# Moving a pool of late buffers by 128 bytes, and the weights of one kind of matmul unit by as much

## The chip, the cores and the metric

The kernel runs on one core of one Trainium2 chip. The metric is the device time of one execution in microseconds (us); the median of several runs counts. Beside the plain runs one execution was profiled, and all durations below are from that one.

## The reference, cut to what matters

A decoder of two layers on 512 tokens of width 1024, in float32. Layer 0 mixes tokens by sliding-window pooling, layer 1 by a gated unit (SGU); each layer ends with an MLP of inner width 4096 that squares a ReLU.

```python
def sgu_mixer(h, w_in, ln_g, ln_b, w_s, b_s, w_out):
    z = jax.nn.gelu(h @ w_in, approximate=False)
    u, v = jnp.split(z, 2, axis=-1)
    v = layernorm(v, ln_g, ln_b)
    ...
    mixed = jnp.einsum('hts,bnshc->bnthc', ws, v) + b_s.T[None, None, :, :, None]
    gated = u * mixed.reshape(B_, S_, SGU_WIDTH)
    return gated @ w_out

def sq_relu_mlp(h, w1, w2):
    return jnp.square(jax.nn.relu(h @ w1)) @ w2

def reference(...):
    for i in range(DEPTH):
        ...
        x = x + g1[:, None, :] * y
        h = modulate(rmsnorm(x, norm_mlp_g[i]), sh2, sc2)
        x = x + g2[:, None, :] * sq_relu_mlp(h, mlp_w1[i], mlp_w2[i])
    return rmsnorm(x, final_g)
```

## The kernel before, in words

**Products.** Every large product is made of float32r matmuls with 128 rows and 128 weight columns. An operand is kept as a high part and a low part (`wh`, `wl` for weights; `hb`, `as`, `o` or `gt` hold both parts of an activation), and `mm3` (L187) issues three matmuls for one product: low weights by high operand, high by low, high by high. In each, TensorE loads 128 columns of one operand as its weights (the trace calls this PEld) and then streams the other, the moving operand, through them, 256 or 512 columns wide.

**Stages, in order of time.** Head and layer 0's mixer (0 to 60 us); a sweep over seven slices of the first MLP weight and one more such slice (`f_run`) with 512 moving columns (60 to 105 us); the first MLP product of layer 0 (105 to 222 us); the second (222 to 385 us); the SGU of layer 1, in which `v` comes first (385 to 431 us), then `u` mixed with the chunk products (431 to 483 us), then the output product (483 to 531 us); the first MLP product of layer 1 (531 to 694 us); the second (694 to 845 us); the last norm and the stores.

**First MLP product.** It is done by a scheme with seven products in place of eight, so it runs in units `("s", (c, j, m))`: `c`, `j` name a block of 256 inner columns (eight blocks) and `m` is 1 to 7. The text calls a unit with `m` = 1 an M1 unit. A unit is 24 matmuls of 256 columns into one PSUM bank (`s_run`, L772). The weights are what `split` (L175) writes: ScalarE copies a raw block to `wh`, VectorE writes the rest to `wl`. The moving operand is `asums.of[m]`: for `m` = 1, 2, 4 and 7 a quarter of the activation `H` (tile `hb`), for `m` = 3, 5 and 6 a sum of quarters (tile `as`). The order in a block is `ORDER` = 1, 5, 6, 3, 2, 7, with 4 of a block set behind the M1 unit of the next one. The bank names in the trace give the unit that opened the bank: `b301q` takes 1, 6, 7 and 4 of block (3, 0), `b305q` takes 5 and 3, `b302q` takes 2.

**Second MLP product.** Units `("p", (c, m))` of 48 matmuls with 512 columns: the weights are the activation `o`, the moving operand is `wh` or `wl` (`p_run`, L860).

**SGU.** For `v` the weights are 128 tokens of `H` and the moving operand is `wh` or `wl`; for `u` it is the other way round, as in the sweep; for the output product the weights are `gt` and the moving operand `wh` or `wl`. All have 512 columns.

**Order.** TensorE's order is that of the program text. The other engines' order is set by the lists of units, with `AHEAD` (5) as the number of units whose weights are prepared ahead. There are five buffers each for `wh` and `wl` and three (`w4`) for raw blocks. GpSimd's queue and SyncE's issue the DMAs.

**Where the buffers lie.** `slot` (L131) takes tags P0 to P3, R0 to R2, S6 and S7 from the pool `big` and all other tags from the pool `late` (L619), which is opened when the pools of the head are closed. `shift` (L100) puts a tile that nothing uses ahead of a pool's others. A buffer of `wh` or `wl` has 1024 + 64 words, so that `split(r, n, at)` can write its 1024 words `at` words behind the buffer's start; `at` is `UNDER` = 16 words (64 bytes) for the units `s` and 0 elsewhere. All buffers of a pool that matter here are a multiple of 256 bytes long, so one number per pool tells where they start modulo 256, in a partition:

| pool | holds | first byte | start modulo 256 |
|---|---|---|---|
| `big` | tags P, R, S6, S7, `gb` | 8320 | 128 |
| `w4` | raw weight blocks | 90240 | 128 |
| `wts` | `wh`, `wl` | 102528 | 128 |
| `late` | tags S0 to S5, T0 to T2 | 154368 to 228096 | 0 |

In layer 0, `H` (`hb`) lies in P0 to P3, that is in `big`. From the start of layer 1 on it lies in S0 to S3, that is in `late` (`hparts` in `normed`, L990 and L993). The sums `as` lie in R0 to R2 and `o` in R0 and R1, in `big`, in both layers. Of `gt` the first half lies in S4 and S5 (`late`), the second in S6 and S7 (`big`). T0 to T2 take raw weight blocks, columns of the modulation matrices and the SGU's constants.

Of the kernel before, what the change touches and what calls it, by code (L numbers as in the profile page):

```python
# [24 lines left out]

LATE = 5

UNDER = 16

LEAD = 4  # L30

# [52 lines left out]
def decoder_kernel(ctx: ExitStack, tc: tile.TileContext, xtok, vecs, rows, fgrow, ada0, adag, ada1, pool_w, w1s, w1f, w1b, w2, w_v, w_u, w_o, wsT, lnp, bs, out):  # L84
# [15 lines left out]
    def shift(pool, words):  # L100

        if words % LINE:
            pool.tile([P, words % LINE], F32, name="shift", tag=f"shift{len(shifts)}", bufs=1)
            shifts.append(words)
# [3 lines left out]
    def f32(t):  # L108
        return t.bitcast(F32)
# [19 lines left out]
    late = []  # L129

    def slot(tag, shape, name, dt=F32):  # L131

        pool = big if tag in ("P0", "P1", "P2", "P3", "R0", "R1", "R2", "S6", "S7") else late[0]
        return pool.tile(shape, dt, name=name, tag=tag)
# [37 lines left out]
    def wpair(at=0):  # L172
        return tuple(wtile(tag)[:, at : at + D] for tag in ("wh", "wl"))

    def split(r, n=1, at=0):  # L175

        h, l = wpair(at)
        for q in range(n):
            c = slice(D // n * q, D // n * (q + 1))
            A.activation(h[:, c], r[:, c], AF.Copy)  # L180
            V.tensor_tensor(l[:, c], r[:, c], f32(h[:, c]), ALU.subtract)  # L181
        return h, l
# [87 lines left out]
    with (  # L270
# [14 lines left out]
        m = band.rearrange("p n g w -> p (n g) w")  # L285
        G.affine_select(out=m, in_=m, compare_op=ALU.is_ge, fill=0.0, base=0, pattern=[[0, 8], [1, W]], channel_multiplier=-1)
        for g in range(4):
            m = band[:, :, g]
# [328 lines left out]


    late.append(ctx.enter_context(tc.tile_pool(name="late", bufs=1)))  # L619


    ORDER = (1, 5, 6, 3, 2, 7)
# [47 lines left out]
    def mlp(i, extra, units, final):  # L670
# [59 lines left out]
        def in_gb(c, j, r, n):  # L730
            return ((r, n) == (1, 0) and (i, c, j) != (1, 0, 0)) or (i, r, n, j) == (1, 1, 1, 1) and c < 2

        def blk(c, j, r, n):
            if (c, j, r, n) not in blks:
                if in_gb(c, j, r, n):
                    assert spare.pop(0) == (c, j, r, n)
                    t = blks[c, j, r, n] = gbs.pop() if gbs and i == 0 else big.tile([P, D], F32, name=f"raw{c}{j}{r}{n}q", tag="gb")
                    nc.sync.dma_start(t, w1b[i, 2 * c + j, r, n])
                else:
                    blks[c, j, r, n] = raw4(w1b[i, 2 * c + j, r, n], f"raw{c}{j}{r}{n}q")  # L740
            return blks[c, j, r, n]
# [4 lines left out]
        def s_prep(u):  # L746
            c, j, m = u

            def b(r, n):
                return blk(c, j, r, n)  # L750

            def add(o, r, n):
                G.dma_start(o, w1b[i, 2 * c + j, r, n], accum_op=ALU.add)

            t = b(0, 0)
            if m in (5, 6):
                V.tensor_tensor(t, t, b(*CHAIN[m]), ALU.add)
            if m == 5:
                add(b(0, 1), 1, 1)
            wb = b(1, 1) if m == 3 else b(1, 0) if m == 2 else b(0, 1) if m == 7 else t  # L760
            w = split(wb, 1, UNDER)
            if m == 6:
                add(t, *CHAIN[4])
            for at in more.get(u, ()):
                blk(*at)
            if spare and (u == ss_[0] or in_gb(c, j, *{2: (1, 0), 3: (1, 1)}.get(m, (0, 0)))):
                blk(*spare[0])
            return w
# [140 lines left out]

        run_ = {"f": f_run, "s": s_run, "p": p_run}  # L910
        prep = {"f": f_prep, "s": s_prep, "p": p_prep}
        calls = dict(sum=sum_up, tl=t_load, bl=b_load, cl=chain, a=asums.step, put=put, sq=squares, xl=lambda h: reload(h, XT[h]))
        items = {"f": 1, "s": 1, "p": 2}
# [169 lines left out]
    wb = [slot(f"T1{n}", [P, HEADS, P], "wsbs") for n in range(2)]  # L1083
# [231 lines left out]
```

## Time and profile before

| what | value |
|---|---|
| runs | 859.76, 864.25 and 868.32 us; median 864.25 |
| the profiled execution's own time | 858.99 us |
| its span, first to last instruction | 857.2 us |
| busy: TensorE matmuls / weight loads | 827.7 us (97%) / 727.3 us (85%) |
| busy: VectorE / ScalarE / GpSimd | 689.5 us (80%) / 514.0 us (60%) / 116.8 us (14%) |
| granted TensorE clock, mean | 0.997 |
| DMA | 188.62 MB, 220 GB/s over the span |

Matmuls overlap in the pipeline, so that the length of one (some 276 or 390 ns) says little of the rate. The rate is read from how many start in a stretch. The chain of waits is followed back from the last instruction; where a row of it is a run of matmuls, TensorE itself was the bound there, and the row's length divided by its count is the time from one matmul to the next.

### The profile page before, as it was taken

Reading aid. Unit: us, or ns where it says so; the run is one execution under the profiler, and the core shown is the slowest. Engines: PE = TensorE matmul, PEld = TensorE weight load, DVE = VectorE, ACT = ScalarE, POOL = GpSimd, SP = SyncE. Lnnn points to the kernel's source line nnn. Section 1 sums busy time; section 2 is a strip of 40 time slices with the busy share of each in tenths; the row PEclk is TensorE's granted clock in tenths of the full one; section 3 lists DMA queues with packets and bytes.
Section 4 is the critical chain, followed back from the end, with each engine's and each line's share of the span. In section 5 each row is a group of like instructions: output and inputs, shape, how many; then the busy total and the mean of one; then the engine's idle time right before and its main releaser. Section 6 shows DMA issues by size and latency. Waiting matters only on the chain.

```text
span 857.2 us, 12735 instructions
## 1 busy us (share of the span) xinstructions
PE 827.7 (97%) x4895; PEld 727.3 (85%) x4895; DVE 689.5 (80%) x878; ACT 514.0 (60%) x738; POOL 116.8 (14%) x135
## 2 busy tenths in 40 slices
PE   8999999999999999989999999999999999999995
PEld 7778898999888888768888777989999988888884
DVE  6889888999689868786898854788787677976886
ACT  5286876667655654656231436868776776655562
POOL 3010001000223210040010001011000032321000
PEclk9999999999999999999999999999999999999998
DMA  9999868899999979354757733558989699999502
GB/s 347 406 349 326 257 186 238 266 298 290 304 216 182 211 215 263 119 188 160 248 191 269 238 107 101 155 152 189 294 238 271 171 223 246 185 214 233 156 14 85
DMA packets 51651, 188.62 MB, mean 220 GB/s; under 512 B 5739, under 2 KB 5891, under 8 KB 50566
## 3 DMA queue, kind: packets, MB, share of 16 engines
q1 hardware_dynamic: 37090, 133.52, 43.3%
q0 software_dynamic: 14352, 54.02, 32.7%
q8 instruction: 38, 0.62, 0.3%
q10 hardware_dynamic: 148, 0.27, 0.1%
q14 instruction: 23, 0.19, 0.1%
HBM read 181.49 MB, written 6.30 MB: 219 GB/s over the span
## 4 chain that ended last, share of the span: by engine, by line
PE 63%; DVE 15%; DMA 11%; issue 5%; ACT 4%; POOL 1%; SPq 0%; DVEq 0%; POOLq 0%; ACTq 0%
PE pm L874 29%; PE po L193 8%; DVE wl L181 4%; PE b211q L193 3%; PE b301q L193 3%; DMA wh<-in_ada 2%; DVE ada L217 2%; PE b201q L193 2%; PE b311q L193 2%; DMA ada<-in_ada 2%; PE b111q L193 1%; PE b315q L193 1%; PE b305q L193 1%; PE b205q L193 1%; PE b215q L193 1%
## 5 line engine op out<-in xcount | busy, mean ns | idle before, releaser
L874 PE MATMUL pm<-wh,o 128*128 128x512 f32 x864 | 214.9, 390 | 3.5 <-DVE o L638 3.1
L874 PEld LDWEIGHTS pm<-wh,o 128*128 128x128 f32 x864 | 161.4, 188 | 39.1 <-DVE o L638 4.4
L874 PE MATMUL pm<-wl,o 128*128 128x512 f32 x432 | 115.6, 389 | 0.0
L180 ACT ACTIVATE wh<-bt 128x1024 fp32r<-128x1024 f32 x64 | 67.2, 1058 | 51.8 <-PE pm L874 43.3
L874 PEld LDWEIGHTS pm<-wl,o 128*128 128x128 f32 x432 | 81.0, 188 | 17.2 <-DVE wl L181 0.4
L181 DVE TENSOR_TENSOR wl<-bt,wh 128x1024 fp32r<-128x1024 f32 x64 | 77.5, 1220 | 19.3 <-ACT wh L180 19.2
L638 DVE TENSOR_TENSOR o<-g,o 128x1024 fp32r<-128x1024 f32 x56 | 68.2, 1219 | 5.6 <-ACT o L637 5.5
L217 DVE SCALAR_TENSOR_TENSOR ada<-ada,cb 128x1024 f32<-128x1024 f32 x56 | 68.1, 1218 | 5.5 <-DMA ada<-in_ada 5.5
L193 PE MATMUL po<-hb,wh 128*128 128x512 f32 x224 | 69.8, 392 | 0.0
L637 ACT ACTIVATE o<-g 128x1024 fp32r<-128x1024 f32 x56 | 58.7, 1048 | 9.5 <-PE pm L874 9.1
L180 ACT ACTIVATE wh<-b 128x1024 fp32r<-128x1024 f32 x32 | 34.0, 1063 | 37.5 <-PE pm L874 37.5
L181 DVE TENSOR_TENSOR wl<-b,wh 128x1024 fp32r<-128x1024 f32 x32 | 39.2, 1224 | 21.3 <-ACT wh L180 21.3
L853 POOL DMA_DIRECT2D bt<-in_w x48 | 41.6, 904 | 106.5 <-DVE wl L181 84.8
L180 ACT ACTIVATE wh<-raw 128x1024 fp32r<-128x1024 f32 x33 | 35.0, 1059 | 33.7 <-PE pm L874 13.8
L181 DVE TENSOR_TENSOR wl<-raw,wh 128x1024 fp32r<-128x1024 f32 x33 | 40.3, 1222 | 15.2 <-ACT wh L180 15.1
L193 PEld LDWEIGHTS po<-hb,wh 128*128 128x128 f32 x224 | 42.1, 188 | 9.3
L193 PE MATMUL po<-hb,wl 128*128 128x512 f32 x112 | 44.5, 397 | 0.0
L193 PE MATMUL po<-wh,gt 128*128 128x512 f32 x128 | 41.1, 398 | 1.0 <-DVE gt L1152 1.0
L692 ACT ACTIVATE g<-g 128x512 f32<-128x512 f32 (+1 forms) x72 | 41.1, 600 | 1.2
L193 PE MATMUL po<-wh,hb 128*128 128x512 f32 x128 | 40.5, 395 | 0.0
L797 ACT ACTIVATE g<-g 128x512 f32<-128x512 f32 x42 | 26.2, 624 | 16.7 <-DVE g L791 7.9
L193 PEld LDWEIGHTS po<-wh,gt 128*128 128x128 f32 x128 | 24.1, 188 | 7.4 <-DVE gt L1152 2.1
(447 smaller groups left out, 1996.2 us busy)
## 6 DMA issues: line engine op xcount, KB each, us to landing
ada<-in_ada SPq DMA_DIRECT2D x72, 512.0 KB, 4.9
bt<-in_w POOLq DMA_DIRECT2D x48, 512.0 KB, 9.6
bt<-in_w SPq DMA_DIRECT2D x16, 512.0 KB, 6.8
raw<-in_w SPq DMA_DIRECT2D x16, 512.0 KB, 7.2
b<-in_w SPq DMA_DIRECT2D x16, 512.0 KB, 9.9
b<-in_w POOLq DMA_DIRECT2D x16, 512.0 KB, 9.9
wh<-in_ada SPq DMA_DIRECT2D x9, 512.0 KB, 9.9
wl<-in_ada SPq DMA_DIRECT2D x9, 512.0 KB, 9.9
```

Of the source, the lines that this page charges most:

```text
L180: A.activation(h[:, c], r[:, c], AF.Copy)
L181: V.tensor_tensor(l[:, c], r[:, c], f32(h[:, c]), ALU.subtract)
L193: T.matmul(o[:, c], a, b[:, c], start=first and q == 0 and not c.start, stop=last and q == 2 and c.stop is None, **kw)
L217: keep(V.scalar_tensor_tensor(r, r, 1.0, cb, ALU.mult, ALU.mult, accum_out=pmv[i, b][:, j : j + 1]))
L637: A.activation(o[0], a, AF.Copy)
L638: V.tensor_tensor(o[1], a, f32(o[0]), ALU.subtract)
L692: A.activation(t, t, AF.Square)
L797: A.activation(t, t, AF.Relu)
L853: G.dma_start(r, piece(c, *nxt, q), accum_op=ALU.add)
L874: T.matmul(banks[hf], o[a][:, 2 * q + p, hf], w[q][b][:, S * p : S * p + S], start=start and q + n + p == 0, stop=stop and q + n + p == 4, ...
```

## The change

The pool `late` begins with an unused tile of `PAD` = 32 words (128 bytes), so that each of its buffers lies 128 bytes further on. M1 units write and read their weights `RESET` = 48 words (192 bytes) behind the buffer's start in place of 16 words (64 bytes). No instruction is added, removed or moved; only addresses differ.

```diff
 LATE = 5
 
+PAD = 32
+
 UNDER = 16
+
+RESET = 48
...
     late.append(ctx.enter_context(tc.tile_pool(name="late", bufs=1)))
+    shift(late[0], PAD)
...
             wb = b(1, 1) if m == 3 else b(1, 0) if m == 2 else b(0, 1) if m == 7 else t
-            w = split(wb, 1, UNDER)
+            w = split(wb, 1, RESET if m == 1 else UNDER)
```

## The prediction

> **What bounds the kernel now.** I read the page first, then the chain of waits.
>
> ```profile
> span 857.2 us, 12735 instructions
> PE 827.7 (97%) x4895; PEld 727.3 (85%) x4895; DVE 689.5 (80%) x878; ACT 514.0 (60%) x738; POOL 116.8 (14%) x135
> ...
> PE 63%; DVE 15%; DMA 11%; issue 5%; ACT 4%; POOL 1%; SPq 0%; DVEq 0%; POOLq 0%; ACTq 0%
> ```
>
> TensorE is busy 97% of the span, but only 63% of the chain that ends last is TensorE's. A faster matmul is worth its time in that part alone. In the two MLPs the chain, in order of time, has these rows (start us, length us, what, count):
>
> ```profile
> 67.28 3.40 PE po L193 x15
> ...
> 200.90 2.72 PE b311q L193 x24
> 203.62 2.72 PE b301q L193 x24
> ...
> 263.02 81.66 PE pm L874 x360
> ...
> 605.28 2.83 PE b101q L193 x24
> ...
> 652.72 2.83 PE b301q L193 x24
> 655.54 2.83 PE b211q L193 x24
> 658.37 2.73 PE b305q L193 x24
> 661.10 2.72 PE b301q L193 x24
> 663.82 2.72 PE b305q L193 x24
> 666.54 2.83 PE b302q L193 x24
> 669.36 2.83 PE b301q L193 x24
> 672.19 2.83 PE b311q L193 x24
> 675.02 2.83 PE b301q L193 x24
> ...
> 732.73 92.31 PE pm L874 x407
> ```
>
> The reader is to see two rates for one kind of unit. All `b` rows are 24 matmuls of the same shape, yet some take 2.72 us (113 ns a matmul) and others 2.83 us (118 ns). The row at 203.62 is unit 4 of block (3, 0) in layer 0, the row at 675.02 the same unit in layer 1: 2.72 against 2.83. In layer 1 the units on `as` (5, 6 and 3: the rows at 658.37, 661.10, 663.82) have 2.72, and those on `hb` (1, 4, 2, 7) 2.83. Matmuls of 512 columns run at 81.66 / 360 = 227 ns and 3.40 / 15 = 227 ns.
>
> What differs is where the two operands lie. Let d be the start of the next matmul's weights, which load while a matmul streams, less the start of the moving operand, modulo 256. From the table of pools: layer 0's units have weights at 128 + 64 and `hb` at 128, d = 64, and so have the `as` units of both layers. Layer 1's units on `hb`, which lies at 0 in `late`, have d = 192. The sweep and the second products have d = 0. In the SGU, `v`, `u` and the first half of `gt` have d = 128:
>
> ```profile
> 385.10 8.37 PE po L193 x36
> ...
> 395.22 11.17 PE po L193 x48
> ...
> 406.42 1.07 ACT wh L180
> ...
> 454.44 7.40 DMA ada<-in_ada
> ...
> 481.80 5.58 DMA raw<-in_w_o
> ...
> 493.81 24.58 PE po L193 x105
> ```
>
> 8.37 / 36 and 11.17 / 48 give 233 ns, against 227 ns of the sweep, which is the same line with the same shape at d = 0. The chain is on TensorE up to 406.42, then goes by VectorE, ScalarE and DMA until 493.81.
>
> The offset alone does not settle the rate. Windows of layer 0 (length, TensorE busy and count, clock, DMA share, GB/s) and one of layer 1:
>
> ```profile
> 104.98:124.53 19.55, 19.55 (x168) 1.00 0.65 177
> 164.00:222.00 58.00, 58.00 (x514) 1.00 0.90 282
> 543.30:548.30 5.00, 5.00 (x47) 1.00 0.35 94
> ```
>
> A window's count holds two or three matmuls begun before it. At d = 64 both times, 166 in 19.55 us are 118 ns and 512 in 58 us are 113 ns. In the third window, d = 192, some 44.5 in 5 us are 112 to 113 ns. So each offset can run at either rate, and a rate stays until a stop of TensorE or a change of d. The slow stretch of layer 0 ended at such stops (the longest one in each row, then the SGU's):
>
> ```profile
> PE b101q L193 <- DVE g L793: 1.2, 1, 1.2
> ...
> PE b111q L193 <- DVE g L793: 0.8, 1, 0.8
> PE po L193 <- DVE gt L1152: 1.0, 1, 1.0
> ```
>
> Where d goes from 192 to 64 without a stop, the next unit is fast within a few matmuls: 2.73 at 658.37, behind 2.83 at 655.54. On the way back it is slow at once: 663.82 fast, 666.54 slow. The chain shows this at each such change behind 569 us.
>
> **The change, part by part.** No instruction or DMA is added or moved and no queue is passed. Only d changes, in four places.
>
> (1) Layer 1, units 2, 4 and 7: `hb` moves from 0 to 128, so d goes from 192 to 64. On the chain from 569 to 694 us TensorE is without a gap; there 20 units of that kind stand at 2.83 us. They become 2.72: 20 x 0.11 = **-2.2 us**. The four M1 units there keep d = 192 (both operands move) and stay at 2.83. Ahead of 569 us the units wait for VectorE, and a faster one only waits longer: 0. What is behind, the second product, takes the gain on, since ScalarE there waits for TensorE and not for data:
>
> ```profile
> L180 ACT ACTIVATE wh<-bt 128x1024 fp32r<-128x1024 f32 x64 | 67.2, 1058 | 51.8 <-PE pm L874 43.3 <-DMA bt<-in_w 5.8 <-DVE tmp L951 2.7
> ```
>
> 43.3 us of its waits are on TensorE and 5.8 on DMA.
>
> (2) SGU: d goes from 128 to 0, the sweep's. Up to 406 us: 84 matmuls x (232.6 - 226.7 ns) = -0.5. From 493.81: 105 x 226.7 ns = 23.8 for 24.58, less a slow restart in it: -0.6. Together **-1.1 us**. Between, 108 matmuls of `v` and 192 of `u` would save 300 x 5.9 ns = 1.8 us of TensorE's time, but the chain there is VectorE and DMA, and TensorE waits at the end (1.0 us for `gt`). I count 0 and keep 1.8 for the range: if it all lies on the path, it counts in full.
>
> (3) Layer 0's M1 units: d goes from 64 to 192. Nearest row: layer 1's M1 units, 2.83. On the gapless stretch behind 146 us these are the units at 162.82, 181.86 and 200.90: 3 x 0.11 = **+0.3 us**. Bounds: 0 (the third window is fast at 192) and +0.3. The other units keep d = 64; by (1)'s rows the step from 192 to 64 leaves them fast.
>
> (4) The slow stretch at 105 to 125 us would end early, but VectorE is what TensorE waits for right behind it: 0 here. Where an execution has no lucky stop and stays slow at d = 64 up to 214 us, the rows from 146.22 to 211.78 are 25 units, 25 x 0.11 = 2.8 us more; M1 units at d = 192 would end that. How often it happens no trace here shows: bounds 0 and -2.8; I take -1.
>
> ScalarE, VectorE and DMA now meet `late` at 128 instead of 0. Blocks split from `late` and from `w4`, which already lies at 128, take the same, and DMAs into both land alike:
>
> ```profile
> L181 DVE TENSOR_TENSOR wl<-bt,wh 128x1024 fp32r<-128x1024 f32 x64 | 77.5, 1220 | 19.3 <-ACT wh L180 19.2
> ...
> L181 DVE TENSOR_TENSOR wl<-raw,wh 128x1024 fp32r<-128x1024 f32 x33 | 40.3, 1222 | 15.2 <-ACT wh L180 15.1
> ...
> ch11q<-in_w1b SPq DMA_DIRECT2D x2, 512.0 KB, 6.0
> ...
> raw1101q<-in_w1b SPq DMA_DIRECT2D x2, 512.0 KB, 6.9
> ```
>
> So 1220 against 1222 ns and 6.0 against 6.9 us: 0.
>
> **Sum**: -2.2 - 1.1 + 0.3 = -3.0 us against the profiled execution's own 858.99: 856.0. That execution is 5.3 us under the median of the runs, 864.25. The four known times (858.99, 859.76, 864.25, 868.32) have the mean 862.8, which I take as what an execution of the kernel before gives. 862.8 - 3.0 - 1 = **859 us**.
>
> The Trainium skill speaks against all of this: "TensorE: Matmul & The Clock Gate", Part 2, says that TensorE has two independent read ports and that loading the next weights takes no bandwidth from the running matmul, so an address could not matter. By that rule the sum would be 0. The rows at 203.62 and 675.02 disagree with it: one shape, 2.72 and 2.83 us. Its result is the time of rival C below, and has C's chance.
>
> **The rivals.** *More of it lands* (B): the SGU's middle is on the path after all and layer 0's slow rate is frequent in plain runs: 862.8 - 3.0 - 1.8 - 2.8 = 855.2. For it: TensorE's waits there are small (1.0 us), and the runs spread over 8.6 us. Against: the chain's rows at 454.44 and 481.80 are DMA.
>
> *It does nothing* (C): not the offset but the operand's place decides, `late` against `big`; layer 1's slow units all stream from `late`. Then units 2, 4 and 7 stay at 2.83 and M1 units of layer 0, in `big`, at 2.72: 858.99, or 862.8 as a plain run. For it: this trace never has `hb` in `late` at 128. Against: the fast window at 543 us streams from `late`.
>
> *M1 units spread the slow rate* (D), the slower one: the offset is a phase, and a unit entered at 192 leaves those behind it slow at 64, as in the window at 105 us. In layer 0 that is 16 units behind the three M1 units, +1.8, with the M1 units +0.3; in layer 1 the 12 `as` units behind 610.94, +1.3, while only the six units ahead of it gain, -0.7; SGU -1.1: +1.6, 860.6, or 864.4 as a plain run. It decides from 27 slow units of the 42 on (3.0 / 0.11). Against: every change from 192 to 64 in this trace ends fast.
>
> **How the numbers follow.** Forecast 0.46 (own range 856 to 863), B 0.29, C 0.12, D 0.10, something else 0.03. About 1% is what a measurement of this kernel tells from no change: under 855.6 is faster, over 872.9 slower. Faster: 0.20 of B, 0.11 of the forecast by the runs' spread, 0.01 of C: 0.32. Slower: 0.04 of D, 0.01 of C, 0.03 of the rest: 0.08. Within: 0.60. Range 853 (B with some spread) to 866 (D with some).
>
> **What would show it.** In the chain of the changed kernel: rows 2.72 for units 2, 4 and 7 of layer 1, 2.83 for M1 units of both layers alone; `po` rows of the SGU at 227 ns a matmul; the first units at 105 us fast behind the M1 ones. Rows of 2.83 on `as` units are D; 2.83 on `b302q` is C; a longer wait for `gt` shows the SGU's middle hidden. The forecast is wrong if the late buffers' new place slows a DMA or VectorE, or if the stops fall so that another rate is caught.

## The result, and the profile after

| | before | after |
|---|---|---|
| median of the runs side by side, us (16 each) | 861.9 | 857.32 |
| lowest to highest, us | 859.12 to 868.32 | 850.98 to 866.2 |
| the profiled execution: own time, span, mean granted clock | 858.99, 857.2, 0.997 | 866.2, 864.5, 0.987 |

The ratio of after to before, which compares means and leaves out the one slow execution among the changed kernel's 16 (866.2 us, the profiled one), is 0.9933, with 95% of its uncertainty between 0.9906 and 0.9960. The changed kernel is faster by 0.7%, some 5.8 us between these means and 4.6 us between the medians. The forecast was 859.0 us in a range of 853 to 866, and "within 1%" as the likeliest class. A second set of 12 runs of the changed kernel, beside other runs of the kernel before, gives 0.9945 (0.9913 to 0.9978).

The profiled execution of the changed kernel holds three pieces at half the clock, so its spans say little; rows of full clock in it do, and a second profiled execution (858.5 us, below) stands beside it.

The page of the changed kernel:

```profile
span 864.5 us, 12735 instructions
PE 829.7 (96%) x4895; PEld 730.2 (84%) x4895; DVE 689.5 (80%) x878; ACT 513.5 (59%) x738; POOL 115.6 (13%) x135
...
PE 57%; DVE 18%; DMA 13%; issue 6%; ACT 4%; POOL 1%; SPq 0%; DVEq 0%; POOLq 0%; ACTq 0%
```

The instruction counts are the same, and VectorE's busy time too (689.5 us in both): the new place of `late` costs VectorE nothing. TensorE's share of the chain went from 63% to 57%. Its chain of waits (start us, length us, what, count; the lines of the code have moved on by four or five, so that L193 is L197 and L1152 is L1157):

```profile
391.30 8.16 PE po L197 x36
...
401.21 10.91 PE po L197 x48
...
482.88 5.33 DMA raw<-in_w_o
...
660.78 2.72 PE b301q L197 x24
663.50 2.72 PE b211q L197 x24
666.22 2.72 PE b305q L197 x24
...
674.38 2.72 PE b302q L197 x24
677.10 2.72 PE b301q L197 x24
679.82 2.72 PE b311q L197 x24
682.54 2.72 PE b301q L197 x24
```

These are the rows that stood in the prediction from 652.72 on. Every unit of layer 1 has 2.72 us there, also those that had 2.83: units 2, 4 and 7 (674.38, 663.50 and 677.10), as forecast, and the M1 units (660.78 and 679.82), which the forecast left at 2.83. The SGU's `po` rows are at 8.16 / 36 = 10.91 / 48 = 227 ns a matmul, where they had 233. Ahead of the output product the chain still goes by a DMA.

TensorE's waits on `gt` (us in total, times, longest), 1.0 us before:

```profile
PE po L197 <- DVE gt L1157: 4.2, 2, 3.1
```

The wait is longer, which the prediction gave as the sign that the SGU's faster middle is hidden. How far this sign holds is taken up with the experiment on the SGU.

Two windows of layer 0 (length, TensorE busy and count, granted clock, DMA share, GB/s):

```profile
148.60:162.70 14.10, 14.10 (x122) 1.00 0.85 274
165.80:179.00 13.20, 13.20 (x119) 1.00 0.83 278
```

Less the two or three matmuls begun before a window, the first has some 119.5 in 14.10 us, 118 ns each, and the second 116.5 in 13.20 us, 113 ns. Between them, at 162.8 us, lies an M1 unit, amid work without a gap. In the kernel before, a slow stretch at constant offsets had ended only where TensorE stopped. A short stop was enough: by the starts of its matmuls the slow stretch that began at 105 us ended at 124.9 us, where one matmul came 221 ns behind the last in place of 118; the stop of 1.2 us that the prediction shows for it came later, at 131.6 us, when the rate was 113 ns already. Here an M1 unit at 192 bytes ended such a stretch without any stop.

### The profile page after: what moved, and what is told of

Its sections match the earlier page's. It is cut to its first block, busy times and chain, and to the rows that moved or that the text cites. A ratio compares the mean times of both kernels' runs of the same rounds, so it can differ in the third digit from the quotient of the medians.

```text
span 864.5 us, 12735 instructions
## 1 busy us (share of the span) xinstructions
PE 829.7 (96%) x4895; PEld 730.2 (84%) x4895; DVE 689.5 (80%) x878; ACT 513.5 (59%) x738; POOL 115.6 (13%) x135
## 4 chain that ended last, share of the span: by engine, by line
PE 57%; DVE 18%; DMA 13%; issue 6%; ACT 4%; POOL 1%; SPq 0%; DVEq 0%; POOLq 0%; ACTq 0%
PE pm L879 29%; PE po L197 6%; DVE wl L185 4%; PE b211q L197 3%; PE b301q L197 3%; DMA ada<-in_ada 2%; DMA wh<-in_ada 2%; DVE ada L221 2%; PE b201q L197 2%; PE b311q L197 2%; DVE ada L401 1%; PE b111q L197 1%; PE b205q L197 1%; ACT wh L184 1%; PE b315q L197 1%
## 5 line engine op out<-in xcount | busy, mean ns | idle before, releaser
L879 PE MATMUL pm<-wh,o 128*128 128x512 f32 x864 | 217.1, 393 | 5.2 <-DVE o L643 3.1
L197 PE MATMUL po<-hb,wh 128*128 128x512 f32 x224 | 69.0, 389 | 0.0
L197 PEld LDWEIGHTS po<-hb,wh 128*128 128x128 f32 x224 | 42.1, 188 | 8.5
L197 PE MATMUL po<-wh,gt 128*128 128x512 f32 x128 | 42.4, 408 | 4.2 <-DVE gt L1157 4.2
L197 PE MATMUL po<-hb,wl 128*128 128x512 f32 x112 | 44.1, 394 | 0.0
L197 PE MATMUL po<-wh,hb 128*128 128x512 f32 x128 | 39.8, 390 | 0.0
L197 PEld LDWEIGHTS po<-wh,gt 128*128 128x128 f32 x128 | 25.3, 197 | 10.4 <-DVE gt L1157 5.0
```

The lines of the kernel that those rows point to most:

```text
L197: T.matmul(o[:, c], a, b[:, c], start=first and q == 0 and not c.start, stop=last and q == 2 and c.stop is None, **kw)
L879: T.matmul(banks[hf], o[a][:, 2 * q + p, hf], w[q][b][:, S * p : S * p + S], start=start and q + n + p == 0, stop=stop and q + n + p == 4, ...
```

## The experiments

Each edit is to the changed kernel. Beside the ratio, a second reading is given. Each run lists the mean clock granted to TensorE, c; (1 - c) x span is the time that the withheld clock costs if all of it delays the end. Over the 35 runs of the kernel before that stood beside the first four experiments the time rises with it by 1.02 us for each us (correlation 0.67). Taken off each run, it leaves a mean with less noise. A part of it is the end of the kernel, where each profiled execution has half clock and TensorE hardly any work (from 851.6 us on in the kernel before). The clocks are given to 0.001, 0.9 us, so single runs are not read by it.

| kernel | runs | median, us | ratio to before (95%) | mean less the withheld clock, us |
|---|---|---|---|---|
| before | 35 | 861.38 | 1 | 856.6 ± 0.4 |
| after | 16 | 857.32 | 0.9933 (0.9906 to 0.9960) | 851.6 ± 0.6 |
| after, again (e6) | 12 | 857.79 | 0.9945 (0.9913 to 0.9978) | 852.3 ± 0.65 |
| pad alone (e1) | 12 | 858.94 | 0.9983 (0.9954 to 1.0013) | 853.5 ± 0.6 |
| reset alone (e2) | 12 | 860.62 | 0.9996 (0.9972 to 1.0020) | 856.4 ± 0.35 |
| same differences, no pad (e3) | 12 | 859.08 | 0.9974 (0.9954 to 0.9994) | 854.0 ± 0.5 |
| after, SGU as before (e4) | 12 | 858.72 | 0.9964 (0.9931 to 0.9997) | 853.9 ± 0.5 |
| after, waits filled (e5) | 12 | 862.17 | 1.0003 (0.9968 to 1.0039) | 856.1 ± 0.9 |
| after, reset often (e9) | 12 | 856.84 | 0.9950 (0.9927 to 0.9973) | 851.5 ± 0.4 |

The ± is one standard error. Both sets of the changed kernel together have 851.9 ± 0.45; without the 866.2 us execution the first has 851.4. The experiments ran on three chips: e1 to e4 on one, e5 to e8 on a second, e9 on a third. The kernel before has 856.6, 856.3 and 856.2 on them by the last column, so a difference between two chips has some 0.4 us more doubt than its ±. By the ratio alone, pad alone, reset alone and the filled kernel can't be told from the kernel before.

### Pad alone, and reset alone

```diff
-            w = split(wb, 1, RESET if m == 1 else UNDER)
+            w = split(wb, 1, UNDER)
```

> Late buffers 128 bytes further on, but M1 units with their weights at 64 bytes as before: every unit of the first MLP products has d = 64. By the theory that the difference d decides (T1): all layer 1 units from about 580 us on take 2.72 us, M1 units too, the SGU runs at 227 ns, and layer 0 behaves as before, slow (2.83 us) from its first unit to the first stop of TensorE that happens to end it; 0 to 3 us slower than the changed kernel, 3 to 6 us faster than before. By the theory that the place decides (T2: streaming from the pool late is slow): layer 1's units on hb stay at 2.83 us and the time is that of before. By the theory that the M1 units' other offset is what puts an end to a slow stretch (T3): a slow stretch, wherever one begins, lasts over M1 units to the next stop of TensorE; the changed kernel's trace has one that ended at an M1 unit (145.8 to 165.7 us).

```diff
-    shift(late[0], PAD)
```

> Late buffers where they were, M1 units with their weights at 192 bytes. T1: layer 0 as in the changed kernel; in layer 1 the M1 units now have d = 64 (weights at 64, hb at 0) and take 2.72 us, units 2, 4 and 7 keep d = 192 and 2.83 us; the SGU keeps 233 ns. 0 to 3 us faster than before, 3 to 5 us slower than the changed kernel. T2: as before within 1 us. T3: no slow stretch of layer 0 lasts past an M1 unit; layer 1 as before.

**Measured.** 858.94 us and 860.62 us. The pad alone is worth 3.1 ± 0.75 us by the last column, the M1 units' offset alone 0.2 ± 0.5, both together 4.7 ± 0.6. The pad alone: a unit of layer 1 that had 2.83 (the M1 unit of block (2, 1)), from the chain, and then the first units of layer 0 in a window of TensorE (length, busy and count, clock, DMA share, GB/s). Third, a window of TensorE at the same place of the changed kernel:

```profile
633.72 2.72 PE b211q L197 x24
```

```profile
106.00:125.60 19.60, 19.60 (x168) 1.00 0.65 177
```

```profile
107.20:123.40 16.20, 16.20 (x145) 1.00 0.57 167
```

The gapless part of layer 1 is all at 2.72 without any M1 offset. But the stretch from 105 us on, where these units begin, is as slow as in the kernel before, 166 in 19.60 us or 118 ns, up to TensorE's next stop. The changed kernel has some 142.5 in 16.20 us there, 114 ns: by the starts of its matmuls the first unit, an M1 unit, is slow and the ones behind it are fast. This is no accident of one execution: in all seven traces with layer 0's M1 units at 192 bytes (both of the changed kernel, reset alone, same differences, SGU as before, waits filled, reset often) the first unit at 105 us has 118 ns and those behind it 113 to 114; in the two with 64 bytes (before, pad alone) all seven units there have 118. So the pad gives layer 1 its rate, and the M1 offset ends slow stretches. On top of the pad that is worth 853.5 - 851.9 = 1.6 ± 0.8 us, by runs of different chips.

The reset alone, from the chain: two rows of layer 0, then some of layer 1:

```profile
164.43 2.83 PE b211q L197 x24
167.26 2.72 PE b201q L197 x24
...
658.60 2.72 PE b301q L197 x24
661.32 2.72 PE b211q L197 x24
664.04 2.83 PE b305q L197 x24
...
678.18 2.83 PE b311q L197 x24
681.01 2.83 PE b301q L197 x24
```

In layer 0, where `hb` lies at 128 with and without the pad, the M1 unit at 164.43 is the last unit at 2.83 us behind a stop at 147 us, and the units at 2.72 follow it without a gap, as in the changed kernel. In layer 1 `hb` lies at 0. The unit on `as` at 664.04 lies exactly as in the kernel before, with d = 64, and had 2.73 there (658.37). Here it has 2.83, as have the two `as` units behind it. A unit's own addresses do not settle its rate.

### The same differences at other places

No pad. The weights of units 2, 4 and 7 of layer 1 go 128 bytes up in its place, and the SGU's weights too, so that every d is that of the changed kernel, or 0 in the SGU, but the moving operands lie where they lay before:

```diff
-    shift(late[0], PAD)
...
-            w = split(wb, 1, RESET if m == 1 else UNDER)
+            w = split(wb, 1, RESET if (m == 1 if i == 0 else m in (2, 4, 7)) else UNDER)
...
-        wv = blocks(w_v[ch])
+        wv = blocks(w_v[ch], (PAD,) * 4)
...
-                wu[q] = split(ur[q // 2][:, q % 2])
+                wu[q] = split(ur[q // 2][:, q % 2], 1, PAD)
...
-        wo = blocks(w_o[dh])
+        wo = blocks(w_o[dh], (PAD, PAD, 0, 0))
```

> Late buffers where they were; in place of moving them, the weights that meet them are moved: SGU weights 128 bytes behind their buffers' start (the output product's only where gt lies in late), layer 1's units 2, 4 and 7 at 192 bytes, its M1 units at 64 bytes, layer 0's M1 units at 192 bytes. Every d is that of the changed kernel, and hb is still at 0 in late. T1: the changed kernel's time within 2 us, 3 to 8 us faster than before; SGU 227 ns, units 2, 4 and 7 at 2.72 us. T2: layer 1's hb units stay at 2.83 us, SGU at 233 ns, time of before within 1 us.

**Measured.** 859.08 us, 854.0 by the last column, between the kernel before and the changed one. The chain of this kernel:

```profile
385.84 8.17 PE po L197 x36
...
395.76 10.91 PE po L197 x48
...
654.02 2.72 PE b211q L197 x24
656.74 2.83 PE b305q L197 x24
659.57 2.83 PE b301q L197 x24
662.39 2.83 PE b305q L197 x24
665.22 2.74 PE b302q L197 x24
667.97 2.72 PE b301q L197 x24
```

At 512 columns the difference decides: the SGU's rows are at 227 ns with both operands moved, in another place than in the changed kernel, at d = 0. At 256 columns it doesn't: units 4, 2 and 7 (654.02, 665.22, 667.97) and the three units on `as` between them all have d = 64, and the former are fast and the latter slow.

Four kernels differ in whether an operand's offset changes from unit to unit in layer 1 (rates of the gapless part, in one execution each):

| kernel | weights | moving operand | layer 1 |
|---|---|---|---|
| before | stay at 192 | 0 and 128 by turns | `as` 2.72, `hb` 2.83 |
| pad alone | stay at 192 | stays at 128 | all 2.72 |
| after | 192, M1 64 | stays at 128 | all 2.72; in a second execution 16 units of 2.83 first |
| same differences | 192 and 64 by turns | 0 and 128 by turns | `as` 2.83, `hb` 2.72 to 2.74 |

So slow and fast units take turns without a stop only where the **moving operand's** offset changes. Where that stays at 128, the rate of 113 ns holds through the changes of the weights' offset; the rate of 118 ns begins only behind a stop (the second execution, below) or with the stage, and ends at a stop or at an M1 unit with another offset. Not shown is whether the change does it or the place 0 itself: the prediction's window at 543 us is fast with the moving operand at 0, but it is short, and no kernel here keeps that operand at 0 over a whole gapless part. Which of the two turns is the slow one differs between the first and the last row, and the reset alone shows a mix; for that I have no rule.

### The SGU put back, and its share

The changed kernel with the three SGU edits of the last diff: `hb` and half of `gt` lie 128 bytes up, the SGU's weights follow or lead by 128, and d is 128 in the SGU again.

```diff
-        wv = blocks(w_v[ch])
+        wv = blocks(w_v[ch], (PAD,) * 4)
...
-                wu[q] = split(ur[q // 2][:, q % 2])
+                wu[q] = split(ur[q // 2][:, q % 2], 1, PAD)
...
-        wo = blocks(w_o[dh])
+        wo = blocks(w_o[dh], (PAD, PAD, 0, 0))
```

> The changed kernel, but the SGU's weights 128 bytes behind their buffers' start where they meet late buffers, so that d is 128 there again. T1: the SGU is back at 233 ns; what the changed kernel gained there is lost: 1.1 us if only the stretches on the chain count, 2.9 us if the middle counts too. T2: as the changed kernel, within 0.5 us. The units of layer 1 stay at 2.72 us by either.

**Measured.** 858.72 us. Its chain:

```profile
387.28 8.39 PE po L197 x36
...
397.41 52.99 PE po L197 x228
...
485.55 33.15 PE po L197 x144
```

The rate is 8.39 / 36 = 233 ns again. With this kernel each of the four placements of 512-column matmuls has run: weights and moving operand both at 0, or both at 128, give 227 ns, and one at 0 and the other at 128, either way round, 233.

In this execution the chain of the SGU is on TensorE alone, from 397 us to its end, with no wait on `gt`. The rate does not settle that: the kernel before and the reset alone, at 233 ns too, have VectorE and DMA in the chain there and wait 1.0 and 1.8 us for `gt`. At 227 ns the wait is 4.2 and 3.2 us in the two executions of the changed kernel, 1.9 in the pad alone, 1.8 in the reset often and 0.7 in the same differences. So the wait is longer with the faster rate on the whole, and part of the 1.8 us that the faster middle saves seems to end in it, but single executions overlap. By the last column the SGU is worth 853.9 - 851.9 = 2.0 ± 0.65 us. That lies between the 1.1 that was forecast and the bound of 2.9, and rules out neither. What is left against the reset alone, which has the same SGU rate, is layer 1's first MLP product: 856.4 - 853.9 = 2.5 ± 0.6 us.

### Filling TensorE's waits

The changed kernel's trace shows a granted clock of a half in three pieces (length, then busy and count of TensorE, its weight loads, VectorE, ScalarE and GpSimd, the clock, DMA share, GB/s):

```profile
374.50:381.30 6.80, 5.82 (x21) 5.09 (x22) 4.10 (x6) 5.46 (x8) 0.00 (x0) 0.50 0.51 180
494.00:500.80 6.80, 5.46 (x13) 4.30 (x14) 5.98 (x12) 3.01 (x5) 0.00 (x0) 0.50 0.84 249
237.90:241.40 3.50, 2.84 (x7) 2.27 (x8) 3.50 (x4) 1.55 (x2) 1.49 (x2) 0.51 0.99 187
```

The first begins in the last 0.4 us of a wait of 2.4 us for `xs`, the second in the longest wait for `gt`, 3.1 us, and the third in a wait of 1.4 us. The kernel before waits as long for `xs` at the same place, at full clock (its row of waits, and a window of TensorE from the end of this one on):

```profile
PE px L998 <- ACT xs L986: 3.1, 2, 2.4
```

```profile
371.00:380.00 9.00, 7.99 (x43) 1.00 0.73 264
```

So such a wait does not bring half clock each time. If it does so at times, and costs clock as well as its length, then filling it should help. Ten matmuls whose results nothing uses were put into the wait for `xs` and the two for `gt`:

```diff
+FILL = (5, 2, 3)
...
+            if (i, n, hf, k) == (1, 0, 0, 0):
+                fill(px, FILL[0])
...
+                if (dh, t) == (0, 0) and k in (6, 7):
+                    fill(bank("fill"), FILL[k - 5])
```

> The changed kernel with ten more float32 matmuls of 256 columns (two passes of 215 ns each, results unused): five, 2.2 us, ahead of the transposes that wait 2.4 us for the scaled rows at the end of layer 0; two and three, 0.9 and 1.3 us, ahead of the two products in the SGU's output that wait for the last two gt. If TensorE's waits there are what halves the granted clock afterwards (half clock begins at 374.5 and at 494.0 us in the changed kernel's trace, right behind or in these waits), the granted clock of the runs rises from a mean that loses 5.9 us of the span to one that loses about 3, and the time falls by 2 to 3 us against the changed kernel. If half clock comes for another reason, the clock stays and the time is the changed kernel's, or up to 2 us more where a wait was shorter than the added work.

> The changed kernel itself, beside the others of this set: 0.9933 of before within 0.003, and the loss by half clock between that of before and 1 us more.

**Measured.** The filled kernel has 862.17 us, 1.0003 (0.9968 to 1.0039) of the kernel before: the gain is lost. Its waits:

```profile
PE px L1012 <- ACT xs L998: 2.1, 2, 1.4
PE po L204 <- DVE gt L1166: 1.9, 1, 1.9
```

The waits became shorter, 2.1 for 3.0 and 1.9 for 4.2 us, and half clock still followed them, at 372.43 and 488.48. By the last column it is 3.9 ± 1.1 us slower than the changed kernel on the same chip. The fills take some 4.3 us (20 passes of 215 ns) and the waits became 3.2 us shorter in the one execution that was profiled; where the rest is lost is not shown. Whether they were too few or of the wrong kind, or fills cannot prevent this, stays open.

The changed kernel again, 857.79 us. From its second profiled execution, the chain, the wait for `gt` and a window at the SGU's start:

```profile
609.33 2.83 PE b111q L197 x24
612.16 2.83 PE b201q L197 x24
614.98 2.72 PE b101q L197 x24
...
634.02 2.72 PE b211q L197 x24
```

```profile
PE po L197 <- DVE gt L1157: 3.2, 1, 3.2
```

```profile
372.30:375.70 3.40, 3.40 (x15) 3.11 (x14) 3.35 (x5) 3.04 (x6) 0.00 (x0) 0.50 0.38 137
```

Here a stop at 569 us left layer 1 in the slow rate, for 16 units, up to the first M1 unit of layer 1's gapless stretch, at 612.16. That unit is still slow itself, and the next one, with the weights back at 192, is fast. The half clock is there in this execution too, in a shorter piece. Half clock does not tell the kernels apart: the time it withholds has a mean of 5.2 us in the 35 runs of before, of 5.9 and 5.6 in the two sets of after, and of 5.6 in the runs of before beside the second set.

### All units at one difference of 0, or of 128

The 256-column units with the weights of all seven kinds at 0 words, or at 32, in place of 16 and 48, so that d is 0, or 128, everywhere:

```diff
-UNDER = 16
+UNDER = 0
...
-RESET = 48
+RESET = 0
```

> The changed kernel with all weights of the first MLP products at their buffers' start, M1 units too: d = 0 in every unit, and no offset ever changes. If d sets the rate: that of the last 24 matmuls of 256 columns at d = 0 in the trace of before, 120 ns, so 2.88 us a unit in all stages, some 13 us more than the changed kernel over both layers (84 units x 0.16). If a change of the moving operand's offset sets it (T4): 113 ns from the first or second stop of TensorE on, and the changed kernel's time within 3 us.

```diff
-UNDER = 16
+UNDER = 32
...
-RESET = 48
+RESET = 32
```

> The changed kernel with all weights of the first MLP products 128 bytes behind their buffers' start, M1 units too: d = 128 in every unit. If d sets the rate as in the SGU before (233 against 227 ns at d = 128): 116 ns or more a matmul, 2.8 to 2.9 us a unit, 6 to 15 us more. By T4: 113 ns behind a stop, or slow from one stop to the next, as at d = 64; within 4 us of the changed kernel.

**Measured.** One run each: 866.94 and 864.08 us, 9 and 6 us above the changed kernel's median on that chip, 857.79. The chains, first at 0 in layer 1, then at 128 in layer 0 and layer 1:

```profile
627.45 2.88 PE b201q L197 x24
...
633.21 2.88 PE b202q L197 x24
```

```profile
152.50 2.88 PE b201q L197 x24
...
625.43 2.85 PE b201q L197 x24
...
631.13 2.85 PE b202q L197 x24
```

At 0 each unit of the gapless parts of both layers has 2.88 / 24 = 120 ns. At 128 those of layer 0 have 2.88 as well, 120 ns, and those of layer 1 2.85, 119 ns (119.9 and 118.6 by the starts of the matmuls). The rows at 152.50 and 625.43 are the same unit on `as`, with the same starts modulo 256 in both layers, so this difference too has two rates, only closer ones. No unit comes near 113 ns though nothing alternates: theory T4 is wrong for these two differences, and d has a part in the rate. Of the four differences that ran, 64 and 192 alone show the rates of 113 and 118 ns. For 512 columns it is another order: 0 is the fast one there (227 ns) and 128 the slow one (233).

### A reset in every second unit

```diff
-            w = split(wb, 1, RESET if m == 1 else UNDER)
+            w = split(wb, 1, RESET if m in (1, 3, 5, 7) else UNDER)
```

> The changed kernel with the weights at 192 bytes in units 1, 3, 5 and 7 instead of 1 alone, so that nearly every second unit changes the weights' offset; the moving operands stay at 128. If a unit whose weights come back from 192 to 64 bytes ends a slow stretch (T3), no stretch at 118 ns that a stop begins lasts longer than two or three units, where the changed kernel had them of up to 17; a fast stretch stays fast through all the changes; time that of the changed kernel or up to 2 us less. If a change of the weights' offset itself can start a slow stretch, slow units appear behind changes without a stop of TensorE, and the time is 1 to 5 us more.

**Measured.** 856.84 us, 0.995 (0.9927 to 0.9973): the same as the changed kernel. Its chain:

```profile
612.65 2.72 PE b201q L197 x24
...
628.97 2.72 PE b202q L197 x24
```

On the gapless stretches every unit is fast, from 132 us on in layer 0 and from 567 us on in layer 1 by the starts of its matmuls, and the fast rate holds through all the changes of the weights' offset. Ahead of them, where TensorE stops every few us, five units from 551 to 565 us are slow, more than the two or three expected; the step of the weights back to 192 among them has a stop of 0.08 us in it and ends nothing. The runs lie closer together, 855.15 to 859.75 us. That the time isn't lower fits the small price: the 16 slow units of the second execution above, at 0.11 us each, are 1.8 us in one execution, and M1 units already end such stretches, if later. It beats the kernel before, and the changed kernel by nothing that can be measured.

## Why the prediction was right, and where it was not

The time came out 1.7 us under the forecast, inside its range, with the ratio inside "within 1%" (0.9906 to 0.9960). Before rounding the forecast was 862.8 - 4.0 = 858.8. Against the medians, 861.9 and 857.32, the starting value was 0.9 us too high and the change, -4.6, 0.6 us more than forecast. By the last column the change is -4.7 ± 0.6. So the size was right, but two of the four reasons were not, and that the errors stayed small is in part luck.

**(1) Layer 1, units 2, 4 and 7: size right, reason wrong.** The step was to turn d = 192 into d = 64, and -2.2 was forecast. The rows became 2.72, and layer 1 is worth 2.5 ± 0.6 us. But the step rested on d = 64 being fast and 192 slow with a change between them. The kernel of the same differences has d = 64 in units on `as` at 2.83, and the M1 units at 192 have 2.72 in the changed kernel. What changed in layer 1 is that the moving operand no longer alternates between 0 and 128. The size came out by luck: the same 128 bytes that set d to 64 also put `hb` where `as` lies, and in layer 1 it was this that counted.

**(2) SGU: rate right, size open.** -1.1 was forecast, with the middle at 0 and 1.8 us kept as its bound. It measured 2.0 ± 0.65. The rate, 227 ns, was right. The wait for `gt` grew to 4.2 and 3.2 us in the changed kernel, as the sign said, but to 0.7 to 1.9 us in three other kernels at 227 ns, against none, 1.0 and 1.8 us at 233. In one execution at 233 ns the chain is TensorE's throughout, and there the middle is not hidden; in two it goes by VectorE and DMA. So two bounds lie close together and change places from one execution to the next, and "0" was the low end of 0 to 1.8. Whether the 0.9 us above the forecast are the middle, or noise, is not shown.

**(3) Layer 0's M1 units: wrong.** +0.3 was forecast, from the 2.83 of layer 1's M1 units. Of the three in the gapless stretch, those at 182 and 201 us have 2.72; the one at 162.8 us has 2.82, but as the last unit of a stretch that a stop had made slow, and in the second execution it has 2.72 too. So the offset itself costs nothing, and the true term is the lower bound, 0. By the same mistake the four M1 units of layer 1 were left at 2.83; they are 4 x 0.11 = 0.4 us of step (1)'s 2.5.

**(4) Slow stretches: right in kind.** -1 was taken between 0 and -2.8, for M1 units ending slow stretches. They do: at 162.8 us in the one execution, at 612.16 us in the other, and at 164.43 us in the reset alone. Together with the pad it is worth 1.6 ± 0.8 us; without the pad, 0.2 ± 0.5.

**The rivals.** *It does nothing* (C) falls with the `hb` rows of layer 1, `b302q` among them, at 2.72; its 2.72 for M1 units of layer 0 came true. The Trainium skill's rule of the two independent read ports ("TensorE: Matmul & The Clock Gate", Part 2) gives 0 for this change, and the rows at 2.72, 2.83, 2.85 and 2.88 for one shape of matmul disagree with it. *M1 units spread the slow rate* (D) falls too: they end it. *More of it lands* (B) may be in part what happened: the middle counts by half if the 2.0 us are taken at their mean. The medians, 857.32 and 857.79, lie between its 855.2 and the forecast.

**What stands in place of "d".** For 256 columns d = 0 gives 120 ns and d = 128 119 or 120; at d = 64 or 192 TensorE has two rates, 113 and 118 ns. It keeps the one it has until it stops, when either may come, or until an offset changes. A change of the moving operand's offset can bring the slow rate; a change of the weights' offset, with the moving operand staying at 128, has left the rate of 113 ns as it was, and the step of the weights from 64 back to 192 has turned 118 ns into 113 wherever TensorE ran on without a stop: behind the first unit at 105 us in seven traces, and later in both executions of the changed kernel, in the SGU put back and in layer 0 of the reset alone. With the moving operand at 0 it failed in some: in the reset alone the M1 unit at 678.18 stays slow and so does the one behind. Why is not settled; only starts of matmuls are seen here, no port and no bank.

## What to carry to other kernels

Where one shape of matmul shows two rates in the chain, line up its rows with the start of both operands modulo 256 and with what ran just before: here the choice was worth 113 to 120 ns at 256 columns and 227 to 233 at 512, and the best difference at one width was not the best at the other. Keep the moving operands of one run of matmuls at one offset, and if a slow rate can be caught, let the weights' offset step now and then; on top of the pad that was worth 1.6 ± 0.8 us here. And where TensorE waits only 1 us for VectorE, the next execution may be bound by either: cost a faster matmul there by bounds, not at nothing.

## What the runs showed of the hardware that was not expected

**A change of the weights' offset can reset the rate.** 118 ns a matmul before the M1 unit at 162.8 us and 113 behind it, without a gap; 2.83 and 2.72 us a unit on the two sides of 614.98 us in another execution, and on the two sides of 167.26 us in the reset alone.

**Half clock in and behind short waits.** In all traces, between 60 and 840 us, the pieces have 3.4 or 6.8 us, as in the windows above, and each begins in a wait of TensorE of 1.4 to 3.2 us or up to 0.7 us behind one. The profiled execution of before, with a mean clock of 0.997, has none of them in its middle, though it waits 2.4 us for `xs` too, and neither has that of the same differences; the changed kernel's first has three. What decides is not shown. The withheld clock explains much of the difference between executions of one kernel: 1.02 us of time for each us withheld over 35 runs. The Trainium skill, "TensorE: Matmul & The Clock Gate", Part 1, states a free-running window of 3413 ns that decides between half and full clock; the lengths of 3.4 and twice that agree with it. It speaks of idle gaps over about 3.4 us, and the waits here are shorter: 2.4 us at 374.5.
